# Eight weight sums made by accumulating DMAs instead of VectorE

## The chip, the cores and the metric

The kernel runs on one core of a Trainium2 chip. The metric is the device time of one execution in microseconds (us). Before the change it is 1120.05 us, the median of three runs (1119.95, 1120.05 and 1120.61).

A core has five engines that each work through a queue of their own in order: TensorE (PE, matrix products; its weight loads are shown as PEld), VectorE (DVE), ScalarE (ACT), GpSimd (POOL) and SyncE (SP). SP does no arithmetic here; it only issues DMAs. An instruction that waits for a semaphore holds back all that is behind it on its own engine.

## The reference

One decoder layer for 512 tokens of width 1024, in float32: a gated feed-forward network (FFN1), two attention mixers side by side, a second feed-forward network (FFN2), and a last norm.

```python
h = h + FFN_HALF * _swiglu(_rmsnorm(h, norm_ffn1[i]), ffn1_gate[i], ffn1_up[i], ffn1_down[i])
...                                # mixers
h = h + FFN_HALF * _swiglu(_rmsnorm(h, norm_ffn2[i]), ffn2_gate[i], ffn2_up[i], ffn2_down[i])
return _rmsnorm(h, norm_final)

def _swiglu(x, w_gate, w_up, w_down):
    return (jax.nn.silu(x @ w_gate) * (x @ w_up)) @ w_down
```

The inner width of both networks is 2816. The change concerns the second one's down projection, `ffn2_down`, a matrix of 2816 by 1024.

## The kernel before

**Split products.** Every float32 product is made of three matmuls on a high and a low part of each operand. A weight block (128 rows by 8 tiles of 128) is loaded by SP into a ring of four buffers named `raw` (line 152), ScalarE copies it to `whi` (line 160) and VectorE subtracts to make `wlo` (line 164). TensorE then spends 24 matmuls of 512 columns on a block. Blocks are used strictly in the order in which they are planned. `Weights.prep` issues the load of block i + 3 ahead of the split of block i, and the ring gives a `raw` buffer free when the split of the block four places earlier is done. So SP, which works in order, mostly stands waiting for VectorE's `wlo`.

**FFN1** runs from the start to about 375 us. It takes the 22 blocks of the inner width in three parts of 8, 8 and 6. In each part a loop over `f` makes the gate and up products (two weight blocks to a step, and `swiglu` between), then a loop over `d` makes the eight blocks of the down product.

**A seven-product scheme.** For the first two of these parts FFN2's down product is done with seven products of half blocks instead of eight. It needs sums of quarters of `ffn2_down`. Take a pair of 128-row blocks as a 2 by 2 arrangement b11, b12 (columns 0 to 511 and 512 to 1023 of the first row block) and b21, b22. Four combinations t1 to t4 are wanted of each pair. There are eight pairs. The combinations go to DRAM (`t_sums`) and are read back as weight blocks in FFN2's `down()` at about 800 to 1000 us, beside combinations of the left operand that `gated()` makes.

**Where the sums are made.** This is done ahead of time, in FFN1, by the generator `Weights.early`. The loops of `ffn` call `next(early)` once for each `f`, and at d = 2 and d = 5 of the first two down loops. Step n of it stores the result of item n - 2, loads item n, and works on item n - 1. Items 0 to 11 are weight blocks that are only split ahead (lines 110 and 111). Items 12 to 19 are the eight pairs:

- `load` (line 104): SP issues two DMAs of 512 KB into two `eraw` tiles (four buffers, so two items at a time);
- `work` (line 116): VectorE makes four subtractions of 128x512 into `ehi` and `elo`;
- `store` (line 126): SP issues four DMAs of 256 KB to DRAM.

The load, the work and the store of a step are emitted behind the `swiglu` of that `f`, or behind the addition of that `d`. On SP they stand in one queue with the `raw` loads of line 152. On GpSimd nothing runs between 39 and 349 us.

Of the kernel before, what the change touches and what calls it, by code (L numbers as in the profile page):

```python
# [8 lines left out]
F32 = mybir.dt.float32  # L9
F32R = mybir.dt.float32r  # L10
I32 = mybir.dt.int32
AF = mybir.ActivationFunctionType
OP = mybir.AluOpType
# [42 lines left out]
def f32(ap):  # L56
    return ap.bitcast(F32)


class Weights:  # L60
# [28 lines left out]
    def early(self, pool, sums):  # L89


        nc = self.nc
        order = sorted(self.stored)
        raw, out = {}, {}

        def load(n):
            if n < len(order):
                ap, nk = self.blocks[order[n]]
                raw[n] = [pool.tile([128, nk, 128], F32, name="eraw", bufs=4)]
                nc.sync.dma_start(raw[n][0], ap)  # L100
                return
            raw[n] = [pool.tile([128, 8, 128], F32, name="eraw", bufs=4) for _ in range(2)]
            for t, ap in zip(raw[n], sums[n - len(order)][0]):
                nc.sync.dma_start(flat(t), ap)

        def work(n):
            x, y = out[n] = [pool.tile([128, 8, 128], F32R, name=name) for name in ("ehi", "elo")]
            if n < len(order):
                src, = raw.pop(n)
                nc.scalar.copy(x, src)  # L110
                nc.vector.tensor_tensor(y, src, f32(x), op=OP.subtract)
                return
            (b11, b12), (b21, b22) = (halves(flat(t)) for t in raw.pop(n))
            (t1, t2), (t3, t4) = (halves(flat(f32(t))) for t in (x, y))
            for o, p, q in ((t1, b12, b11), (t2, b22, t1), (t3, b22, b12), (t4, t2, b21)):
                nc.vector.tensor_tensor(o, p, q, op=OP.subtract)

        def store(n):
            x, y = (f32(t) for t in out.pop(n))
            if n < len(order):  # L120
                for part, t in enumerate((x, y)):
                    nc.sync.dma_start(self.stored[order[n]][part], t)
                return
            places = sums[n - len(order)][1]
            for o, t in zip(places, (*halves(flat(x)), *halves(flat(y)))):
                nc.sync.dma_start(o, t)

        total = len(order) + len(sums)
        for n in range(total + 2):
            if n >= 2:  # L130
                store(n - 2)
            if n < total:
                load(n)
            if 1 <= n <= total:
                work(n - 1)
            yield
# [68 lines left out]
def flat(t):  # L205
    return t.rearrange("p a b -> p (a b)")


def halves(t):
    return t[:, :512], t[:, 512:]  # L210
# [159 lines left out]
def layer(ctx, tc, a, out):  # L370
    nc = tc.nc
    tensor, scalar, vector, gpsimd = nc.tensor, nc.scalar, nc.vector, nc.gpsimd
# [18 lines left out]
    def mm(out, lhsT, rhs, start, stop):  # L391
        tensor.matmul(out, lhsT, rhs, start=start, stop=stop)  # L392

    def split(hi, lo, src):
        scalar.copy(hi, src)  # L395
        vector.tensor_tensor(lo, src, f32(hi), op=OP.subtract)
# [276 lines left out]
    with pool("h1") as h_pool, pool("temp1", 2) as temp, pool("tables") as tables, ExitStack() as starting:  # L673
        start = starting.enter_context(pool("start"))
        h = h_pool.tile([128, KD, S], F32, name="h")
        x = start.tile([128, 4, D], F32, name="x")
# [110 lines left out]
    with ExitStack() as mixing:  # L787
# [47 lines left out]
        for k in range(KD):  # L835
            for t in range(4):
                o, ts = kcv_ps[t][:, 0], slice(t * 128, t * 128 + 128)
# [118 lines left out]
        class Turned:  # L956

            o = b = None
# [532 lines left out]
        h = h_pool.tile([128, KD, S], F32, name="h")  # L1491
# [8 lines left out]
        with pool("merge", 2, side="right") as mp:  # L1500
# [9 lines left out]
            for d in range(KD):  # L1510
# [16 lines left out]
                y, z = gates_z  # L1527
# [11 lines left out]
    with pool("temp3", 2) as temp, pool("end") as end:  # L1539
# [18 lines left out]
        def gated(pg, pu, j, pairs):  # L1558
            z = temp.tile([128, S], F32, name="z")
            vector.tensor_tensor(z, pg, r_b, op=OP.mult)  # L1560
            s = temp.tile([128, S], F32, name="s")
            scalar.activation(s, z, AF.Silu)
            t = temp.tile([128, S], F32, name="t")
            vector.tensor_tensor(t, pu, r_b, op=OP.mult)
            if not pairs:
                g = temp.tile([128, 8, 256], F32, name="g").rearrange("p m c -> p (m c)")[:, :S]
                vector.tensor_tensor(g, s, t, op=OP.mult)
                split(G[:, j], G[:, 8 + j], g)
                return
            if j % 2 == 0:  # L1570
                left["g"] = temp.tile([128, 8, 256], F32, name="g")
            g, p = left["g"], j // 2
            o = g[:, 1:3] if j % 2 else g[:, 0:8:7]
            vector.tensor_tensor(o, *(x.rearrange("p (i c) -> p i c", i=2) for x in (s, t)), op=OP.mult)
            if j % 2 == 0:
                return
            if j == 7:
                W.prep(W.pos + 3)
            hi, lo = left_hi[:, p], left["lo"][:, p]
            vector.tensor_tensor(g[:, 3], g[:, 7], g[:, 2], op=OP.add)  # L1580
            scalar.copy(hi[:, 0:4], g[:, 0:4])
            vector.tensor_tensor(g[:, 4], g[:, 3], g[:, 0], op=OP.subtract)
            vector.tensor_tensor(lo[:, 0:4], g[:, 0:4], f32(hi[:, 0:4]), op=OP.subtract)
            vector.tensor_tensor(g[:, 5], g[:, 0], g[:, 7], op=OP.subtract)
            vector.tensor_tensor(g[:, 6], g[:, 1], g[:, 4], op=OP.subtract)
            scalar.copy(hi[:, 4:7], g[:, 4:7])
            vector.tensor_tensor(lo[:, 4:7], g[:, 4:7], f32(hi[:, 4:7]), op=OP.subtract)

        def down():


            home = {1: "acc", 6: "acc", 7: "acc", 5: "o", 3: "o", 2: "s", 4: "s"}
            gets = {1: ((0, 0, 0.5),), 5: ((0, 1, 0.5), (1, 1, 0.5)), 2: ((0, 0, 0.5),), 6: (), 3: ((0, 1, 0.5),),
                    4: ((1, 0, -0.5),), 7: ()}
            more = {6: ((0, 1),), 7: ((1, 0), (1, 1))}
            banks = {}
            u = temp.tile([128, 2, 512], F32, name="u", bufs=1)
            for m, g in STEPS:
                if g == 0:
                    banks[m] = [psum.tile([128, 512], F32, name=home[m]) for _ in range(2)]  # L1600
                wh, wl = (w.rearrange("p (a b) c -> p a (b c)", a=2) for w in W.next())
                for t in range(2):
                    ps, c = banks[m][t], slice(t * 128, t * 128 + 128)
                    for q in range(2):
                        ah, al = (x[:, 2 * g + q, LEFT[m], c] for x in (left_hi, left["lo"]))
                        mm(ps, ah, wh[:, q], g == q == 0, False)
                        mm(ps, al, wh[:, q], False, False)
                        mm(ps, ah, wl[:, q], False, g == q == 1)
                    if g == 0:
                        continue  # L1610
                    if m == 1:
                        scalar.activation(u[:, t], ps, AF.Identity, scale=0.5)
                    if m in more:
                        vector.scalar_tensor_tensor(u[:, t], ps, 0.5, u[:, t], op0=OP.mult, op1=OP.add)
                    for i, k, by in gets[m]:
                        y = o_t[:, 2 * i + t, k * 512:k * 512 + 512]
                        vector.scalar_tensor_tensor(y, ps, by, y, op0=OP.mult, op1=OP.add)
                    for i, k in more.get(m, ()):
                        y = o_t[:, 2 * i + t, k * 512:k * 512 + 512]
                        vector.tensor_tensor(y, y, u[:, t], op=OP.add)  # L1620
            turn[0] = 0

        def residual(d):
# [70 lines left out]
        for third, (f0, f1) in enumerate(THIRDS):  # L1694
            for f in range(f0, f1):
                pg = acc(False)
                mm3(pg, W.next(), u_in, KD, col if f == 0 else None)
                pu = acc(False)
                mm3(pu, W.next(), u_in, KD, rows if f == 0 else None)
                if f < 2:  # L1700
                    for d in range(4 * f, 4 * f + 4):
                        residual(d)
                if f == 1:
                    make_room()
                if third == 2:
                    next(last)
                if third < 2 and f + 1 == f1:
                    W.prep(W.pos + 2)
                gated(pg, pu, f - f0, third < 2)
            if third < 2:  # L1710
                down()
# [27 lines left out]
```

## Time and profile before

| | |
|---|---|
| median of three runs | 1120.05 us |
| span of the profiled execution (first to last instruction) | 1118.3 us |
| what lies around the span, by the median | 1.75 us |
| PE busy | 1103.9 us (99%) |
| DVE busy | 696.0 us (62%) |
| ACT busy | 473.2 us (42%) |
| POOL busy | 155.3 us (14%) |
| granted TensorE clock, mean | 0.999 |

The profiled execution has no time of its own beside its span; the three runs are 1.65 to 2.31 us above that span.

How to read the lines: "L116" is line 116 of the kernel; "ehi<-eraw" is the tile written and the tile read; "x8" is how many there are. In a timeline the first number is the start in us from the start of the span and the second the duration. "DMA to landing" is the time from the issue of a DMA to its completion. SPq rows are DMAs that SP issues. In a table by stretches each engine has its busy us and, in brackets, its instructions; then the granted clock, the mean busy share of the 16 DMA engines, and what they moved in GB/s.

### The profile page before, as it was taken

How to read it: one execution, taken by the hardware profiler on the slowest of the kernel's cores; microseconds unless marked ns; L12 is line 12 of the kernel's file. 1: busy time of each engine (PE TensorE's matmuls, PEld its weight loads, DVE VectorE, ACT ScalarE, POOL GpSimd, SP SyncE). 2: the span in 40 equal slices, each digit the busy share in tenths (PEclk: the TensorE clock that was granted, in tenths of full speed). 3: DMA queues.
4: the chain of work that ended last, by engine and by line, in shares of the span. 5: the costliest groups of instructions: out<-in, count | busy, mean ns of one | idle time of the engine just before them, and what ended most of it. 6: DMA issues, size and time to landing. Idle time of an engine off the chain costs nothing.

```text
span 1118.3 us, 14946 instructions
## 1 busy us (share of the span) xinstructions
PE 1103.9 (99%) x5571; PEld 933.3 (83%) x5571; DVE 696.0 (62%) x1275; ACT 473.2 (42%) x890; POOL 155.3 (14%) x173
## 2 busy tenths in 40 slices
PE   9999999999999999999999999999999999999997
PEld 7888888888888999998888888888888888888876
DVE  5665447674656588896777546653667754685553
ACT  5444223321234456766666543434334322342332
POOL 0100000000001144644233422120000000000002
PEclk9999999999999999999999999999999999999999
DMA  7387557886745524224324255633234623354212
GB/s 232 95 245 249 184 175 239 286 276 208 240 143 151 140 79 116 76 76 142 123 93 144 70 162 162 173 87 111 76 113 144 194 79 112 113 178 124 90 61 76
DMA packets 202049, 163.17 MB, mean 146 GB/s; under 512 B 6836, under 2 KB 177656, under 8 KB 201976
## 3 DMA queue, kind: packets, MB, share of 16 engines
q1 hardware_dynamic: 199304, 157.87, 46.0%
q10 hardware_dynamic: 2672, 4.35, 1.0%
q8 instruction: 44, 0.72, 0.3%
q14 instruction: 29, 0.24, 0.1%
HBM read 133.88 MB, written 28.31 MB: 145 GB/s over the span
## 4 chain that ended last, share of the span: by engine, by line
PE 95%; DVE 2%; ACT 1%; issue 1%; POOL 0%; POOLq 0%; DVEq 0%; ACTq 0%
PE acc L392 37%; PE o L392 27%; PE s L392 27%; PE tp L1430 2%; DVE turn_a L1128 0%; PE tp L392 0%; PE tp L1056 0%; PE tp L721 0%; DVE wlo L164 0%; ACT whi L160 0%; PE tp L1627 0%; PE tp L988 0%; DVE s L1336 0%; POOL sqacc L581 0%; DVE sqacc L1173 0%
## 5 line engine op out<-in xcount | busy, mean ns | idle before, releaser
L164 DVE TENSOR_TENSOR wlo<-raw,whi 128x1024 fp32r<-128x1024 f32 (+2 forms) x189 | 215.5, 1168 | 40.0 <-ACT whi L160 39.8
L160 ACT CAST whi<-raw 128x1024 fp32r<-128x1024 f32 (+2 forms) x214 | 190.1, 919 | 109.0 <-PE acc L392 43.7
L392 PE MATMUL acc<-uh,whi 128*128 128x512 f32 x336 | 133.4, 397 | 0.7 <-ACT turn_a L1247 0.7
L392 PE MATMUL acc<-uh,wlo 128*128 128x512 f32 x336 | 131.3, 391 | 0.0
L392 PE MATMUL acc<-ul,whi 128*128 128x512 f32 x336 | 131.1, 390 | 0.0
L392 PE MATMUL o<-uh,whi 128*128 128x512 f32 x264 | 103.7, 393 | 0.4 <-ACT whi L726 0.4
L392 PE MATMUL o<-ul,whi 128*128 128x512 f32 x264 | 102.8, 390 | 0.0
L392 PE MATMUL o<-uh,wlo 128*128 128x512 f32 x264 | 102.8, 389 | 0.0
L392 PE MATMUL s<-uh,whi 128*128 128x512 f32 x232 | 90.5, 390 | 0.0
L392 PE MATMUL s<-uh,wlo 128*128 128x512 f32 x232 | 90.3, 389 | 0.0
L392 PE MATMUL s<-ul,whi 128*128 128x512 f32 x232 | 90.3, 389 | 0.0
L392 PEld LDWEIGHTS acc<-uh,wlo 128*128 128x128 f32 x336 | 63.1, 188 | 13.8 <-DVE wlo L164 0.4
L392 PEld LDWEIGHTS acc<-uh,whi 128*128 128x128 f32 x336 | 63.1, 188 | 12.9 <-ACT turn_a L1247 1.1
L392 PEld LDWEIGHTS acc<-ul,whi 128*128 128x128 f32 x336 | 63.2, 188 | 11.8
L581 POOL TENSOR_TENSOR sqacc<-sqacc,turn_a 128x512 f32<-128x512 f32 x14 | 18.2, 1300 | 371.0 <-ACT turn_a L580 371.0
L392 PE MATMUL acc<-whi,uh 128*128 128x256 f32 x224 | 65.5, 292 | 1.2 <-ACT whi L160 1.2
L392 PE MATMUL acc<-wlo,uh 128*128 128x256 f32 x224 | 63.3, 283 | 0.1
L392 PE MATMUL acc<-whi,ul 128*128 128x256 f32 x224 | 63.3, 283 | 0.0
L395 ACT CAST G<-g 128x512 fp32r<-128x512 f32 x28 | 17.4, 622 | 101.5 <-DVE g L633 72.3
L392 PEld LDWEIGHTS o<-uh,whi 128*128 128x128 f32 x264 | 49.6, 188 | 11.4 <-ACT whi L726 0.9
L392 PEld LDWEIGHTS o<-uh,wlo 128*128 128x128 f32 x264 | 49.6, 188 | 10.5
L392 PEld LDWEIGHTS o<-ul,whi 128*128 128x128 f32 x264 | 49.6, 188 | 10.2
(343 smaller groups left out, 2324.9 us busy)
## 6 DMA issues: line engine op xcount, KB each, us to landing
raw<-in_ffn_gate_dram SPq DMA_DIRECT2D x42, 512.0 KB, 4.0
raw<-in_ffn_up_dram SPq DMA_DIRECT2D x42, 512.0 KB, 5.2
raw<-in_ffn_down_dram SPq DMA_DIRECT2D x34, 512.0 KB, 5.1
raw<-in_w_in_dram SPq DMA_DIRECT2D x20, 512.0 KB, 4.3
eraw<-in_ffn_down_dram SPq DMA_DIRECT2D x16, 512.0 KB, 7.0
raw<-t SPq DMA_DIRECT2D x16, 512.0 KB, 3.3
eraw<-in_w_in_dram SPq DMA_DIRECT2D x12, 512.0 KB, 7.6
early<-ehi SPq DMA_DIRECT2D x12, 512.0 KB, 5.3
```

What stands on the lines that cost most here:

```text
L160: self.nc.scalar.copy(self.place(i)[0][:, k0:k1], self.raw[i][:, k0:k1])
L164: engine.tensor_tensor(lo, self.raw[i][:, k0:k1], f32(hi), op=OP.subtract)
L392: tensor.matmul(out, lhsT, rhs, start=start, stop=stop)
L395: scalar.copy(hi, src)
L581: gpsimd.tensor_tensor(sqacc, sqacc, sq, op=OP.add)
L1430: tensor.transpose(ps[:w, hd], u.p[:, hd, kb * w:kb * w + w], ident)
```

## The change

The four combinations are formed by DMAs that add to what stands at their destination (`accum_op=OP.add`). They are issued by GpSimd, as are the four stores. They can only add, so the combinations get other signs, and the left operands of FFN2 get the signs to match.

Of a pair, SP now loads the first row block with one DMA (512 KB) into one `eraw` tile and the second row block with two (256 KB each), halves exchanged, into another. So the tiles hold b11, b12 and b22, b21. Then GpSimd issues, in this order: t1 = b11 + b12, with b12 read from DRAM; t3 = b12 + b22, with b22 read from DRAM; t2 = b22 + t1, with t1 read from the tile; t4 = b21 + t2, with t2 read from the tile. The results replace the loaded data, and the stores read from the `eraw` tiles.

```diff
-            raw[n] = [pool.tile([128, 8, 128], F32, name="eraw", bufs=4) for _ in range(2)]
-            for t, ap in zip(raw[n], sums[n - len(order)][0]):
-                nc.sync.dma_start(flat(t), ap)
+            raw[n] = [pool.tile([128, 1024], F32, name="eraw", bufs=4) for _ in range(2)]
+            row1, row2 = sums[n - len(order)][0]
+            nc.sync.dma_start(raw[n][0], row1)
+            for k in range(2):
+                nc.sync.dma_start(halves(raw[n][1])[k], halves(row2)[1 - k])
...
-            (b11, b12), (b21, b22) = (halves(flat(t)) for t in raw.pop(n))
-            (t1, t2), (t3, t4) = (halves(flat(f32(t))) for t in (x, y))
-            for o, p, q in ((t1, b12, b11), (t2, b22, t1), (t3, b22, b12), (t4, t2, b21)):
-                nc.vector.tensor_tensor(o, p, q, op=OP.subtract)
+            t1, t3, t2, t4 = (h for t in raw[n] for h in halves(t))
+            row1, row2 = sums[n - len(order)][0]
+            for o, i in ((t1, halves(row1)[1]), (t3, halves(row2)[1]), (t2, t1), (t4, t2)):
+                nc.gpsimd.dma_start(o, i, accum_op=OP.add)
...
-            places = sums[n - len(order)][1]
-            for o, t in zip(places, (*halves(flat(x)), *halves(flat(y)))):
-                nc.sync.dma_start(o, t)
+            t1, t3, t2, t4 = (h for t in raw.pop(n) for h in halves(t))
+            for o, t in zip(sums[n - len(order)][1], (t1, t2, t3, t4)):
+                nc.gpsimd.dma_start(o, t)
...
-            vector.tensor_tensor(g[:, 3], g[:, 7], g[:, 2], op=OP.add)
+            vector.tensor_tensor(g[:, 3], g[:, 7], g[:, 2], op=OP.subtract)
...
-            vector.tensor_tensor(g[:, 6], g[:, 1], g[:, 4], op=OP.subtract)
+            vector.scalar_tensor_tensor(g[:, 6], g[:, 1], -1.0, g[:, 4], op0=OP.mult, op1=OP.subtract)
...
-            gets = {1: ((0, 0, 0.5),), 5: ((0, 1, 0.5), (1, 1, 0.5)), 2: ((0, 0, 0.5),), 6: (), 3: ((0, 1, 0.5),),
-                    4: ((1, 0, -0.5),), 7: ()}
-            more = {6: ((0, 1),), 7: ((1, 0), (1, 1))}
+            gets = {1: ((0, 0, 0.5),), 5: ((0, 1, 0.5), (1, 1, 0.5)), 2: ((0, 0, 0.5),), 6: (), 3: ((0, 1, -0.5),),
+                    4: ((1, 0, 0.5),), 7: ()}
+            more = {6: ((0, 1, OP.subtract),), 7: ((1, 0, OP.add), (1, 1, OP.subtract))}
```

More of the change, by code (lines that the diff above doesn't have):

```diff
@@ L101, in load @@
                 return
-            raw[n] = [pool.tile([128, 8, 128], F32, name="eraw", bufs=4) for _ in range(2)]
-            for t, ap in zip(raw[n], sums[n - len(order)][0]):
-                nc.sync.dma_start(flat(t), ap)
+            raw[n] = [pool.tile([128, 1024], F32, name="eraw", bufs=4) for _ in range(2)]
[3 more added lines that the diff above has]
+                nc.sync.dma_start(halves(raw[n][1])[k], halves(row2)[1 - k])
         def work(n):
-            x, y = out[n] = [pool.tile([128, 8, 128], F32R, name=name) for name in ("ehi", "elo")]
             if n < len(order):
+                x, y = out[n] = [pool.tile([128, 8, 128], F32R, name=name) for name in ("ehi", "elo")]
                 src, = raw.pop(n)
@@ L112, in work @@
                 return
-            (b11, b12), (b21, b22) = (halves(flat(t)) for t in raw.pop(n))
-            (t1, t2), (t3, t4) = (halves(flat(f32(t))) for t in (x, y))
-            for o, p, q in ((t1, b12, b11), (t2, b22, t1), (t3, b22, b12), (t4, t2, b21)):
-                nc.vector.tensor_tensor(o, p, q, op=OP.subtract)
+            t1, t3, t2, t4 = (h for t in raw[n] for h in halves(t))
+            row1, row2 = sums[n - len(order)][0]
+            for o, i in ((t1, halves(row1)[1]), (t3, halves(row2)[1]), (t2, t1), (t4, t2)):
+                nc.gpsimd.dma_start(o, i, accum_op=OP.add)
         def store(n):
-            x, y = (f32(t) for t in out.pop(n))
             if n < len(order):
+                x, y = (f32(t) for t in out.pop(n))
                 for part, t in enumerate((x, y)):
@@ L1617, in down @@
                         vector.scalar_tensor_tensor(y, ps, by, y, op0=OP.mult, op1=OP.add)
-                    for i, k in more.get(m, ()):
+                    for i, k, op in more.get(m, ()):
                         y = o_t[:, 2 * i + t, k * 512:k * 512 + 512]
-                        vector.tensor_tensor(y, y, u[:, t], op=OP.add)
+                        vector.tensor_tensor(y, y, u[:, t], op=op)
             turn[0] = 0
```

## The prediction

> **What bounds the kernel now.** I read the page's shares first, then the stretches in which the sums are made, then the waits there.
>
> ```profile
> span 1118.3 us, 14946 instructions
> PE 1103.9 (99%) x5571; PEld 933.3 (83%) x5571; DVE 696.0 (62%) x1275; ACT 473.2 (42%) x890; POOL 155.3 (14%) x173
> ```
>
> ```profile
> core 0: us, PE busy (x) PEld busy (x) DVE busy (x) ACT busy (x) POOL busy (x), PEclk, DMA share, GB/s
> 194.00:230.00 36.00, 36.00 (x161) 29.81 (x160) 23.60 (x38) 11.05 (x14) 0.00 (x0) 1.00 0.83 279
> 230.00:257.00 27.00, 27.00 (x121) 22.37 (x120) 17.02 (x26) 6.86 (x8) 0.00 (x0) 1.00 0.82 269
> 257.00:297.00 40.00, 40.00 (x178) 33.15 (x177) 21.41 (x30) 9.30 (x14) 0.00 (x0) 1.00 0.62 201
> 297.00:316.00 19.00, 19.00 (x85) 15.73 (x84) 13.50 (x18) 6.03 (x8) 0.00 (x0) 1.00 0.76 248
> ```
>
> The stretches run from the first load of a pair to its last store. TensorE is busy for the whole of each at a granted clock of 1.00, and GpSimd does nothing. The longest wait that TensorE or its weight loads have for VectorE's split in all of FFN1 is this one:
>
> ```profile
> PEld acc L392 <- DVE wlo L164: 0.4, 1, 0.4
> ```
>
> So relief for VectorE has at most 0.4 us to win there. The DMA engines are the busiest helper, up to 0.83. What can change is a loss: whether weights still come in time through SP's queue.
>
> ```profile
> SPq L152 <- DVE wlo L164: 82.4, 17, 11.3
> ```
>
> That is SP's own wait between 190 and 325 us: it stands waiting until a raw buffer is free. In this kernel SP runs as far ahead as four buffers let it, and no further.
>
> **VectorE's part goes.** One sum before, and the split behind it:
>
> ```profile
> 308.85 0.69 DVE L116 TENSOR_TENSOR ehi<-eraw 128x512 f32<-128x512 f32 x1
> 309.57 0.69 DVE L116 TENSOR_TENSOR ehi<-eraw,ehi 128x512 f32<-128x512 f32 x1
> 310.18 0.68 DVE L116 TENSOR_TENSOR elo<-eraw 128x512 f32<-128x512 f32 x1
> 310.79 0.69 DVE L116 TENSOR_TENSOR elo<-ehi,eraw 128x512 f32<-128x512 f32 x1
> 311.39 2.35 DVE L164 TENSOR_TENSOR wlo<-raw,whi 128x1024 fp32r<-128x1024 f32 x2
> ```
>
> From 308.85 to 311.39 is 2.54 us; eight sums make 20.3 us of VectorE's 696.0. I cost the gain at nothing, since TensorE covers all of it. Late behind it would be the weights' arrival.
>
> **FFN2's signs.** Four add or subtract changes keep their form. The eight g[:, 6] become a three-operand form. Nearest rows: the instruction now, and a three-operand one of twice the width, beside a subtraction of that width at 0.69 above.
>
> ```profile
> L1585 DVE TENSOR_TENSOR g<-g x8: 415/418/420, 786.8 to 978.6; 128x256 f32<-128x256 f32 x8
> 246.23 0.69 DVE L664 SCALAR_TENSOR_TENSOR h<-o,h 128x512 f32<-128x512 f32 x1 [3.61 <-PE o L392]
> ```
>
> Equal price, so nothing.
>
> **DMAs move.** SP issued 2 loads and 4 stores a sum and now issues 3 loads, 24 instead of 48. GpSimd issues 8 a sum, 64 in all: 32 accumulates and 32 stores. SP's shorter list is worth nothing by itself, since SP waits 82.4 us anyway.
>
> **The new wait.** An eraw tile is now in use until its stores have landed. So SP's load of a pair waits for the stores of the pair two before, and behind that load on SP stand the raw loads. GpSimd's queue is a chain within a sum: t1 and t3 are issued, t2 waits for t1 to land, t4 for t2, the last store for t4, and the next sum's t1 stands behind that store. With A for one accumulate from issue to landing and one issue between sums, GpSimd needs 3A + 0.7 us for a sum. The 0.7 is SP's row for issuing (median 709 ns), as GpSimd issues no DMA before. The issue time's bounds, 0.46 and 1.40 us, move the period by less than 0.7 and the answer by five times that, under 3.5 us, inside the range below.
>
> ```profile
> L104 SPq DMA_DIRECT2D eraw<-in_ffn_down_dram x16: 456/709/1398, 193.9 to 295.9; - x16
> DMA to landing us min/median/max: 6.4/7.0/7.4
> ```
>
> ```profile
> L126 SPq DMA_DIRECT2D t<-ehi x16: 422/566/887, 216.0 to 313.7; - x16
> DMA to landing us min/median/max: 3.9/5.0/6.6
> ```
>
> ```profile
> L152 SPq DMA_DIRECT2D raw<-in_ffn_up_dram x7: 368/396/823, 196.8 to 305.1; - x7
> DMA to landing us min/median/max: 3.7/6.0/8.5
> ```
>
> ```profile
> hd<-h SPq DMA_DIRECT2D x8, 256.0 KB, 2.4
> ```
>
> **The price of A.** No accumulate stands in this trace. From below: 2.4 us, a plain 256 KB in a quiet stretch. From above: 8.5 us, the slowest 512 KB raw load here (the landing line covers all raw loads from 190 to 330 us). An accumulate of 256 KB must read the destination besides the source, 512 KB in all, so its nearest row is a 512 KB transfer in the same crowded stretch: 6.0 us. I take A = 6.0; a sum takes 18.7 us.
>
> **The sum.** SP's queue before, and where TensorE begins the block that the last raw load brings:
>
> ```profile
> 193.94 2.72 SPq L104 DMA_DIRECT2D eraw<-in_ffn_down_dram  x2
> 256.46 1.72 SPq L104 DMA_DIRECT2D eraw<-in_ffn_down_dram  x2
> 258.96 0.38 SPq L152 DMA_DIRECT2D raw<-in_ffn_up_dram  x1
> 295.12 1.41 SPq L104 DMA_DIRECT2D eraw<-in_ffn_down_dram  x2
> 296.63 0.42 SPq L152 DMA_DIRECT2D raw<-in_ffn_up_dram  x1
> 308.12 2.00 ACT L160 CAST whi<-raw 128x1024 fp32r<-128x1024 f32 x2
> 322.19 0.39 PE L392 MATMUL o<-uh,whi 128*128 128x512 f32 x1
> ```
>
> The first pair is loaded at 193.94 and landed 7.0 later, at 200.9. Its t4 lands at 200.9 + 18.0 = 218.9, the n-th after it 18.7 n later, and the stores 5.0 after that. The eighth load needs the sixth sum's stores: 218.9 + 5 x 18.7 + 5.0 = 317.4. Before, it was issued at 295.12: 22.3 us late. The block behind it was issued at 296.63, is the second of the pair cast at 308.12, and is first multiplied at 322.19. Of those 25.6 us it needs 6.0 to land, and 1.0 and 1.2 for its two splits (halves of the rows of 2.00 and 2.35), 8.2; 17.3 us are slack. TensorE stalls for 22.3 - 17.3 = 5.0 us. The sixth load (256.46) comes at 280.0, 23.5 late, but its raw block (258.96) is first multiplied at 289.55:
>
> ```profile
> 289.55 0.39 PE L392 MATMUL o<-uh,whi 128*128 128x512 f32 x1
> ```
>
> That is 30.6 us, slack 22.4, a stall of 1.1 which the 5.0 contains. So the span grows from 1118.3 to 1123.3 us. The runs' median lies 1.75 above that span; the same around the new span gives 1125 us, 0.4% slower. The point of turning is A = 5.7 (5.0/18 below 6.0), and each microsecond of A beyond it costs 18 us, three landings in each of six sums. At 8.5 it would be 50 us, 1170; at 2.4 nothing.
>
> **What lies behind it on GpSimd.** Its next work is the first of eight additions of squares:
>
> ```profile
> 349.01 1.34 POOL L581 TENSOR_TENSOR sqacc<-sqacc,turn_a 128x512 f32<-128x512 f32 x1 [309.69 <-ACT turn_a L580]
> ```
>
> The eighth sum's t4 lands at 218.9 + 7 x 18.7 = 349.8; the addition is then due at 354. This costs nothing, barely.
>
> **The rivals.** *Hidden.* With A below 5.7 us SP's lateness stays inside the slack, and the time is 1120. For it: a plain 256 KB store lands in 5.0 us at the median here and in 2.4 in quiet, two accumulates of a sum have both ends on chip, and a delayed SP queue makes the stretch less crowded. Against it: the double reading, and GpSimd's unknown time for issuing. On the price of such a DMA there is a rule in the Trainium skill, "DMA: Bandwidth & Descriptors", section "Anatomy of one DMA — SWDGE (gpsimd) path": about 2.0 us and the bytes at 436 GB/s. By it a plain 256 KB takes an estimated 2.6 us, the sum would be 8.5 us a pair, and this rival would hold with room. No run here shows a DMA of GpSimd's yet.
>
> *The DMA engines run full.* The four stretches carry a share of 0.83, 0.82, 0.62 and 0.76, so 36 x 0.17 + 27 x 0.18 + 40 x 0.38 + 19 x 0.24 = 31 us of all sixteen are free. A share of 0.83 moves 279 GB/s, so a full one 336. The accumulates add 32 x 0.262 MB = 8.4 MB, 25 us, if they cost what a copy does; 50 if double and 75 if triple. Single fits. Triple is 44 us over; less the 17.3 of slack, 27 us, 1147. Against it: the free share lies unevenly but the last stretch to 340 us is quiet. This is what the Trainium skill warns of, on the same page, section "Issuing engines are not separate DMA queues": DMAs of GpSimd's, SP's and ScalarE's queues run on the same 16 engines and interleave. The trace before cannot test it, having nothing on GpSimd's queue.
>
> *Faster.* Only if VectorE held TensorE somewhere; the 0.4 us above is all that the waits give, 1119.6.
>
> **How the numbers follow.** Forecast (SP waits on the chain, A from 5.7 to 8): 0.42, its own range 1121 to 1160. Hidden: 0.41. Engines full: 0.14. Faster: 0.03. About 0.2%, 2.2 us, is what a measurement of this kernel can tell from no change. Then faster 0.03, the same 0.41, slower 0.56. The range goes from 1119, under which only the last case lies, to 1160, which is A = 7.9.
>
> **What would show it.** In the changed kernel the L116 rows of VectorE are gone. SP waits at L104 for DMAs rather than at L152 for wlo, with the eighth pair's load near 317 us. TensorE has idle time ahead of blocks at 290 to 330 us, released by wlo or whi, and in no other place. An accumulate's landing is the number to look at: below 5.7 us TensorE stays without a gap and I am wrong by 5 us; near 8 I am wrong by 40. The prediction also fails if GpSimd's issue takes several microseconds a DMA, for then stores too lengthen the chain.

## The result

The changed kernel takes 1127.55 us, the median of four runs (1125.45, 1127.41, 1127.69 and 1130.25). Before it was 1120.05. The ratio is 1.0068 with a 95% interval of 1.0053 to 1.0082: it is slower by 0.7%. The profiled execution is the longest of the four: its time is 1130.25 us and its span 1128.5, 10.2 us more than the span before.

The page of the changed kernel, first the busy times, then the shares of the chain that ended last:

```profile
span 1128.5 us, 15012 instructions
PE 1108.7 (98%) x5571; PEld 935.2 (83%) x5571; DVE 675.8 (60%) x1243; ACT 473.2 (42%) x890; POOL 201.1 (18%) x237
...
PE 85%; DMA 6%; DVE 3%; issue 3%; ACT 1%; POOL 1%; SPq 0%; POOLq 0%; DVEq 0%; ACTq 0%
```

VectorE has lost 20.2 us of work (696.0 to 675.8), almost exactly the 20.3 of the eight sums, and the kernel is not faster for it. TensorE still does 5571 matmuls, but 6% of the chain that sets the end is now DMA. The busy PE time has grown by 4.8 us with the same matmuls, so some of them ran more slowly.

The table by stretches shows where. Its columns are the busy us of each engine (instructions in brackets), the granted clock, the share of the 16 DMA engines, and GB/s. The stretch in which the sums are made:

```profile
core 0: us, PE busy (x) PEld busy (x) DVE busy (x) ACT busy (x) POOL busy (x), PEclk, DMA share, GB/s
200.00:250.00 50.00, 50.00 (x222) 41.39 (x221) 25.61 (x41) 12.92 (x16) 14.41 (x19) 1.00 0.95 260
250.00:300.00 50.00, 48.32 (x211) 38.77 (x210) 18.09 (x24) 11.87 (x16) 16.43 (x23) 1.00 0.99 257
300.00:350.00 50.00, 47.80 (x204) 38.78 (x203) 22.87 (x29) 14.86 (x20) 14.90 (x21) 0.97 0.95 243
```

From 250 to 350 us TensorE has idle time, in a stretch where it had none. The last row before was:

```profile
300.00:350.00 50.00, 50.00 (x222) 41.44 (x221) 28.46 (x37) 15.70 (x22) 0.98 (x1) 1.00 0.51 156
```

In the last row after, the clock is 0.97 as well. Cut finer, the same columns:

```profile
323.00:326.70 3.70, 2.09 (x10) 1.39 (x8) 0.00 (x0) 0.92 (x1) 0.15 (x1) 1.00 1.14 280
326.70:330.20 3.50, 2.91 (x7) 1.97 (x8) 3.12 (x4) 0.79 (x3) 2.36 (x4) 0.59 1.19 292
```

In the first of these TensorE stands idle for 1.6 us at full clock. In the second it works, but at a granted clock of 0.59. (The DMA share adds up the packets' times and counts each packet in the stretch in which it starts, so it can come out above 1.)

Lining up the same matmul in the two traces gives the whole difference step by step. By the matmul that started at 322.6 us before, the changed kernel is 5.50 us late, gathered between 273 and 323 us of the kernel before in several small stalls. A spell of 3.41 us at half clock follows and makes it 6.82. At 479 us one wait adds 1.02 (7.84), and a second spell at half clock brings it to 9.02. At the last matmul it is 9.15. The stretch from the start of the last matmul to the end of the span is 8.38 us where it was 7.36, another 1.02. Together that is the 10.2 us. The other three runs left no trace, so how their smaller losses divide isn't known.

**What TensorE waited for at 326 us.** SP's waits in the same window as before, 190 to 325 us, with the total, the count and the longest:

```profile
SPq L104 <- DMA t<-eraw: 64.3, 12, 11.5
SPq L154 <- DVE wlo L166: 15.3, 3, 6.1
```

Before, SP waited 82.4 us for VectorE's `wlo`. Now it waits mostly for GpSimd's stores to land. The eighth pair's loads, and the raw load that stands behind them, in SP's timeline (start, duration):

```profile
314.94 0.34 SPq L104 DMA_DIRECT2D eraw<-in_ffn_down_dram  x1
316.01 1.10 SPq L106 DMA_DIRECT2D eraw<-in_ffn_down_dram  x2
317.21 0.56 SPq L154 DMA_DIRECT2D raw<-in_ffn_up_dram  x1
```

and the other end of that raw load, in the timelines of ScalarE, VectorE and TensorE (in brackets the idle time ahead of the instruction and what ended it):

```profile
325.78 1.04 ACT L162 CAST whi<-raw 128x1024 fp32r<-128x1024 f32 x1 [11.28 <-DMA raw<-in_ffn_up_dram]
326.86 1.23 DVE L166 TENSOR_TENSOR wlo<-raw,whi 128x1024 fp32r<-128x1024 f32 x1 [11.10 <-ACT whi L162]
326.88 0.50 PE L394 MATMUL o<-uh,whi 128*128 128x512 f32 x1 [1.79 <-ACT whi L162]
328.14 0.80 PE L394 MATMUL o<-uh,wlo 128*128 128x512 f32 x1 [0.41 <-DVE wlo L166]
```

All four engines stand in one row: the DMA lands, ScalarE starts at once after 11.28 us of nothing, VectorE after it, TensorE after ScalarE. The matmul at 328.14 takes 0.80 us where 0.39 is usual. That is the half clock.

**Why SP's load was late.** GpSimd's timeline for one pair, the sixth:

```profile
296.56 1.86 POOL L118 DMA_DIRECT2D eraw<-in_ffn_down_dram  x2
301.48 0.86 POOL L118 DMA_DIRECT2D eraw<-eraw  x1 [3.06 <-DMA eraw<-in_ffn_down_dram]
309.23 0.86 POOL L118 DMA_DIRECT2D eraw<-eraw  x1 [6.89 <-DMA eraw<-eraw]
309.77 1.97 POOL L128 DMA_DIRECT2D t<-eraw  x3
312.91 0.55 POOL L128 DMA_DIRECT2D t<-eraw  x1 [1.17 <-DMA eraw<-eraw]
313.45 1.86 POOL L118 DMA_DIRECT2D eraw<-in_ffn_down_dram  x2
```

t1 and t3 are issued at 296.56; t2 follows only when t1 has landed, t4 when t2 has, the last store (that of t4) when t4 has, and the next pair stands behind it. The three landings take 4.9, 7.8 and 3.7 us from issue to issue. The prices over all pairs, by the view of that line (count, then ns of one issue at least, median and most):

```profile
L118 POOL DMA_DIRECT2D eraw<-in_ffn_down_dram x16: 896/1161/1289, 201.8 to 333.1; - x16
L118 POOL DMA_DIRECT2D eraw<-eraw x16: 858/862/871, 206.6 to 347.3; - x16
DMA to landing us min/median/max: 3.4/6.9/9.2
```

### The profile page after: what moved, and what is told of

It is laid out like the page before. It is cut to its first block, busy times and chain, and to the rows that moved or that the text cites. A ratio compares the mean times of both kernels' runs of the same rounds, so it can differ in the third digit from the quotient of the medians.

```text
span 1128.5 us, 15012 instructions
## 1 busy us (share of the span) xinstructions
PE 1108.7 (98%) x5571; PEld 935.2 (83%) x5571; DVE 675.8 (60%) x1243; ACT 473.2 (42%) x890; POOL 201.1 (18%) x237
## 4 chain that ended last, share of the span: by engine, by line
PE 85%; DMA 6%; DVE 3%; issue 3%; ACT 1%; POOL 1%; SPq 0%; POOLq 0%; DVEq 0%; ACTq 0%
PE acc L394 33%; PE o L394 24%; PE s L394 23%; DMA eraw<-eraw 5%; PE tp L1432 2%; DMA raw<-in_ffn_up_dram 1%; POOL eraw L118 1%; PE tp L394 1%; DVE turn_a L1130 0%; DVE wlo L166 0%; PE tp L1058 0%; ACT whi L162 0%; PE tp L723 0%; PE tp L1629 0%; DMA t<-eraw 0%
## 5 line engine op out<-in xcount | busy, mean ns | idle before, releaser
L1667 POOL TENSOR_TENSOR o_t<-o_t,g_b 128x512 f32<-128x512 f32 (+1 forms) x5 | 5.9, 1176 | 334.1 <-ACT z L1661 334.1
```

Source lines behind the costliest of these rows:

```text
L1667: gpsimd.tensor_tensor(y, y, g_b[:, cs], op=OP.mult)
```

## The experiments

The theory is that of the prediction: a pair takes GpSimd three landings one after the other, the stores of the pair two before therefore land late, SP waits for them, and the raw loads behind it on SP come late. The main rival is that the DMA engines are simply full. Each kernel was timed in rounds with the kernel before, whose medians were 1120.03 and 1120.00 us on the two chips used.

**More buffers.** Six `eraw` buffers in place of four: the same DMAs, but SP's load of a pair waits for the stores of the pair three before.

```diff
-            raw[n] = [pool.tile([128, 1024], F32, name="eraw", bufs=4) for _ in range(2)]
+            raw[n] = [pool.tile([128, 1024], F32, name="eraw", bufs=6) for _ in range(2)]
```

> The changed kernel with six eraw buffers instead of four; the accumulates, their order and their bytes stay. Buffer wait (my theory: SP's load of a pair is held until the stores of the pair two before have landed, and the raw loads behind it come later than their slack): a load now waits for the pair three before, one chain of 18.7 us earlier, so the eighth load is about 3 us late instead of 20, inside the slack of 17. TensorE has no gap between 250 and 340 us and never a spell at half clock there; 1121 us, the 1 us left being the longer end (next kernels). Full engines (rival: the sixteen DMA engines cannot carry the accumulates beside the weights, share 0.95 to 0.99 from 200 to 350 us): taking the wait away does not make room, raw loads still land late, TensorE keeps most of its 5.5 us of gaps; 1125 to 1128 us.

Measured: 1121.87 us (1121.49 to 1123.83), ratio 1.0020 [1.0011, 1.0029]. The table by stretches of this kernel, its waits of SP, and the eighth pair's load:

```profile
200.00:250.00 50.00, 50.00 (x222) 41.44 (x221) 26.94 (x42) 15.07 (x18) 13.98 (x19) 1.00 1.04 294
250.00:300.00 50.00, 50.00 (x223) 41.40 (x222) 20.62 (x27) 12.69 (x17) 15.41 (x23) 1.00 0.95 255
300.00:350.00 50.00, 50.00 (x222) 41.43 (x221) 24.01 (x31) 15.81 (x22) 14.83 (x21) 1.00 0.95 235
```

```profile
SPq L104 <- DMA t<-eraw: 36.0, 9, 8.2
```

```profile
301.52 0.34 SPq L104 DMA_DIRECT2D eraw<-in_ffn_down_dram  x1
```

TensorE is busy for 50.00 of 50 us in all three, with a DMA share of 0.95 to 1.04, as full as in the changed kernel. A bandwidth limit would have stayed. The wait for the buffer is the cause of FFN1's loss, and SP may wait 36 us in total without harm: what counts is how late a load has become against the slack of the block behind it. The eighth load goes out 6.4 us later than in the kernel before (301.52 against 295.12), in the changed kernel 19.8 us later. The kernel remains 1.8 us slower, which is not in FFN1.

**No chain.** t2 and t4 add a quarter from DRAM, so no accumulate waits for another's result.

```diff
-            for o, i in ((t1, halves(row1)[1]), (t3, halves(row2)[1]), (t2, t1), (t4, t2)):
+            for o, i in ((t1, halves(row1)[1]), (t3, halves(row2)[1]), (t2, halves(row1)[0]), (t4, halves(row1)[1])):
```

> The changed kernel with t2 and t4 each adding a half of the first row block from DRAM instead of the sum before it, so t2 and t4 are not the sums wanted; 32 accumulates of 256 KB as before, none waiting for another. Buffer wait: a sum takes one landing and about 4 us of issuing instead of three landings, 11 us instead of 18.7, and SP's loads are late by under 5 us; no gap, 1121 us. Full engines: the same bytes through the same engines, more crowded if anything; gaps stay, 1125 to 1128 us or more.

Measured: 1123.3 us (1121.45 to 1123.61), ratio 1.0024 [1.0014, 1.0033]. Two stretches:

```profile
200.00:250.00 50.00, 50.00 (x222) 41.40 (x222) 25.95 (x41) 13.14 (x17) 21.21 (x28) 1.00 1.06 300
250.00:300.00 50.00, 50.00 (x222) 41.42 (x221) 21.59 (x27) 14.86 (x19) 17.30 (x24) 1.00 1.10 308
```

The engines carry more than in the changed kernel (300 and 308 GB/s) and one accumulate takes longer to land, 8.2 us at the median against 6.9. Still TensorE has no gap, and the eighth load goes out at 295.52 us, within half a microsecond of the kernel before. So not the number or the price of the accumulates does the harm, but that they wait for each other.

**A fifth accumulate.** t4 adds t2 twice, which puts one more landing into each pair's chain and 12.5% more DMAs on GpSimd.

```diff
-            for o, i in ((t1, halves(row1)[1]), (t3, halves(row2)[1]), (t2, t1), (t4, t2)):
+            for o, i in ((t1, halves(row1)[1]), (t3, halves(row2)[1]), (t2, t1), (t4, t2), (t4, t2)):
```

> The changed kernel with a fifth accumulate per pair, t4 adding t2 a second time behind the first (so t4 is not the sum wanted). Buffer wait: the chain of a pair grows by one landing of about 6 us, from 18.7 to 25, and the eighth load by six times that, 36 us later, all of it beyond the slack; TensorE stalls some 35 us more, 1155 to 1170 us. Full engines: eight accumulates more at 1.6 us of all engines each are 13 us, so at most 1141 us.

Measured: 1156.02 us (1155.01 to 1156.75), ratio 1.032 [1.0306, 1.0334], 28.5 us over the changed kernel. The eighth load and two stretches:

```profile
339.89 0.34 SPq L104 DMA_DIRECT2D eraw<-in_ffn_down_dram  x1
```

```profile
250.00:300.00 50.00, 41.16 (x163) 32.32 (x162) 10.08 (x11) 6.27 (x6) 15.52 (x21) 0.90 0.90 229
300.00:350.00 50.00, 38.21 (x159) 30.03 (x157) 15.98 (x22) 10.77 (x16) 13.22 (x18) 0.90 0.88 225
```

The eighth load moved by 25 us (314.94 to 339.89), not by the 36 that was expected: the added link made a pair about 4 us longer, not 6. The profiled span moved by 26.5 us (1128.5 to 1155.0) and the median by 28.5. The matmul that started at 322.6 us in the kernel before is 31.3 us late here and 5.5 in the changed kernel, 25.8 us more. So past the slack, the lateness of the chain is paid about one for one. The clock is 0.90 in both rows, but the spells of slow clock ahead of that block add little to this: TensorE stands idle for 11.7 us just before it, waiting for its load. The DMA share is lower than in the changed kernel, 0.90 and 0.88: the engines carry less while TensorE loses most. That ends the rival of full engines.

**Copies instead of accumulates.** The same chain with plain copies, so that no sums are made.

```diff
-                nc.gpsimd.dma_start(o, i, accum_op=OP.add)
+                nc.gpsimd.dma_start(o, i)
```

> The changed kernel with plain copies in the place of the accumulates, same sources, destinations, queue and order, so the copies stand where sums should. Buffer wait: a 256 KB copy of GpSimd's lands in about 4.3 us (its stores' median) against 6.9 for an accumulate, so a pair takes 14 us instead of 18.7, the eighth load is not late, no gap in FFN1, and what stays is the price of 64 DMAs on GpSimd, 1121.9 us as with six buffers. If it is not the accumulating but the queue that makes the chain long, copies land in 6 to 7 us too and the time stays at 1127.

Measured: 1123.2 us (1121.64 to 1123.77), ratio 1.0024 [1.0014, 1.0033]. The chained copies' prices, and GpSimd's first and last issue of a pair:

```profile
L118 POOL DMA_DIRECT2D eraw<-eraw x16: 536/536/538, 206.1 to 330.8; - x16
DMA to landing us min/median/max: 2.3/5.1/7.2
```

```profile
202.10 1.33 POOL L118 DMA_DIRECT2D eraw<-in_ffn_down_dram  x2 [162.28 <-DMA eraw<-in_ffn_down_dram]
...
321.28 1.07 POOL L118 DMA_DIRECT2D eraw<-in_ffn_down_dram  x2
```

A pair takes (321.28 - 202.10) / 7 = 17.0 us, not the 14 that was expected: a chained copy lands in 5.1 us here. The accumulating itself, its longer issue included, then costs 1.7 of the changed kernel's 18.7 us a pair, and three landings in a row the rest. The eighth load goes out at 304.12, 9.0 us later than before, inside the slack. TensorE has no gap in FFN1 at 17.0 us a pair and has them at 18.7, which brackets the turning point that the prediction worked out (3 x 5.7 + 0.7 = 17.8 us).

**VectorE without the sums, no accumulates.** Only the loads and GpSimd's stores are left of a pair.

```diff
-            for o, i in ((t1, halves(row1)[1]), (t3, halves(row2)[1]), (t2, t1), (t4, t2)):
-                nc.gpsimd.dma_start(o, i, accum_op=OP.add)
```

> The changed kernel without its 32 accumulates: the row blocks are loaded and stored as they are, no sums are made by any engine. 32 DMAs of GpSimd's are left. Buffer wait: no chain, so no late load, no gap in FFN1. VectorE makes no sums here and made them in the kernel with GpSimd's stores alone (1122.24 us); if VectorE's 20 us are worth nothing, as predicted, the two are equal: 1121 to 1122 us. If VectorE's relief is worth something, it is below 1120.0. The last drain of GpSimd's, which was 0.64 us with 0 DMAs, 3.27 with 32, 5.88 with 64 and 6.54 with 72, is 3.3 us again.

**VectorE with the sums, GpSimd with the stores.** One edit to the kernel before:

```diff
-                nc.sync.dma_start(o, t)
+                nc.gpsimd.dma_start(o, t)
```

> The kernel before, with only its 32 stores of the sums issued by GpSimd instead of SP; VectorE makes the sums. If the longer end of the changed kernel (GpSimd's last drain 5.88 us instead of 0.64, the span's end 8.4 instead of 7.4 us behind the last matmul) comes from GpSimd having issued DMAs at all: the same long drain here, 1121.0 us, no gap in FFN1. If it comes from accumulates or something else: 1120.0 us and a drain of 0.6 us.

Measured: 1122.33 us (1120.46 to 1122.81; ratio 1.0016 [1.0007, 1.0024]) without any sums, and 1122.24 us (1120.6 to 1122.96; 1.0015 [1.0006, 1.0024]) with all sums on VectorE. The two have the same stores on GpSimd and differ by VectorE's 20.3 us, and their times are the same (they ran on different chips, on which the kernel before agrees within 0.03 us). They are the same, too, within each of the two groups into which the runs of both fall: 1120.46 to 1120.89 and 1120.60 to 1120.98 in the lower, 1122.22 to 1122.81 and 1122.24 to 1122.96 in the upper (the last section says what parts them). The relief of VectorE is worth nothing. Neither has a gap in FFN1. But both stand above the kernel before, which the theory of the chain doesn't explain, and the drain at the end is longer in both than before. The last drain of GpSimd's queue (the third figure, in ns) in four kernels: the kernel before,

```profile
L1735 POOLq DRAIN  x3: 34/78/642, 1112.6 to 1118.0; - x3
```

the stores alone on GpSimd (32 DMAs),

```profile
L1735 POOLq DRAIN  x3: 40/93/3274, 1113.5 to 1118.9; - x3
```

the changed kernel (64),

```profile
L1737 POOLq DRAIN  x3: 46/102/5884, 1121.8 to 1128.2; - x3
```

and the fifth accumulate (72):

```profile
L1737 POOLq DRAIN  x3: 46/93/6536, 1147.7 to 1154.8; - x3
```

642, 3274, 5884 and 6536 ns lie on a line: 0.64 us and 0.082 us for each DMA that GpSimd issued at any time in the kernel. At 32 it is hidden beside the last output (last matmul to end of span 7.38 us, before 7.36). At 64 that stretch is 8.38, at 72 9.02. This is the 1.0 us at the end.

**A control without DMAs on GpSimd.** The kernel before with the pairs' stores from ScalarE:

```diff
-                nc.sync.dma_start(o, t)
+                nc.scalar.dma_start(o, t)
```

> The kernel before, with its 32 stores of the sums issued by ScalarE: a control beside the one whose stores GpSimd issues (1122.24 us), with no DMA on GpSimd. If the 0.8 to 1.0 us that all kernels with GpSimd DMAs lose at 479 us (VectorE's 128x2 addition there takes 1.14 instead of 0.16 us beside a running GpSimd instruction) and the rest of the 2 us come from GpSimd's DMAs, this one is at 1120.0 us. If any small shift of FFN1's DMAs brings them, it is at 1121 to 1122 us as well.

Measured: 1120.81 us (1120.55 to 1122.5), ratio 1.0013 [1.0004, 1.0022]. The drain is 0.64 us and the end 7.35, as before, but the loss at 479 us is there: the one wait is 1.0 us longer. The place in the kernel before, in the timelines of GpSimd and VectorE and in its waits:

```profile
472.64 1.28 POOL L164 TENSOR_TENSOR wlo<-raw,whi 128x512 fp32r<-128x512 f32 x1
473.81 0.16 DVE L1340 TENSOR_TENSOR e<-m,sink 128x2 f32<-128x2 f32 x1
```

```profile
PE s L392 <- ACT pbuf L1344: 0.8, 1, 0.8
```

and in the control:

```profile
473.50 1.28 POOL L164 TENSOR_TENSOR wlo<-raw,whi 128x512 fp32r<-128x512 f32 x1
473.66 1.14 DVE L1340 TENSOR_TENSOR e<-m,sink 128x2 f32<-128x2 f32 x1
```

```profile
PE s L392 <- ACT pbuf L1344: 1.8, 1, 1.8
```

The VectorE instruction of two columns takes 1.14 us in place of 0.16. It stands in the chain that leads to ScalarE's `pbuf`, for which TensorE now waits 1.8 us and not 0.8. The changed kernel has the same instruction at 1.15 us and the same wait of 1.8. Beside it GpSimd makes a row of 128x512 subtractions. In the control VectorE's instruction starts 0.16 us into one of them and ends as that one ends, at 474.8. In the kernel before it starts 1.17 us into a subtraction of 1.28 us, and also ends as that one ends, at 473.9 to 474.0. In all nine versions other than the kernel before, the control among them, it starts 0.15 to 0.19 us into a subtraction and takes 1.13 to 1.15 us. The Trainium skill states, in "SBUF — State Buffer", section "Who interferes with whom", that VectorE and GpSimd share a pair of ports under an exclusive lock, and that a VectorE instruction with two SBUF inputs contends with a GpSimd instruction that reads SBUF. The rows agree with it. So this part belongs to the phase of the two engines, which every edit of FFN1's queues here moved. Why it moves was not tried.

**Buffers and SP's stores together.** The accumulates stay, with six buffers and the stores back on SP, one step later so that SP needn't wait for t4.

```diff
-            raw[n] = [pool.tile([128, 1024], F32, name="eraw", bufs=4) for _ in range(2)]
+            raw[n] = [pool.tile([128, 1024], F32, name="eraw", bufs=6) for _ in range(2)]
...
-                nc.gpsimd.dma_start(o, t)
+                nc.sync.dma_start(o, t)
...
-        for n in range(total + 2):
-            if n >= 2:
+        for n in range(total + 3):
+            if 2 <= n < len(order) + 2:
                 store(n - 2)
...
+            if n >= len(order) + 3:
+                store(n - 3)
```

> The changed kernel with six eraw buffers and the stores of the sums back on SP, one step later than before so that SP seldom waits for the chain; only the accumulates stay on GpSimd, 32 DMAs. The version that keeps the sums off VectorE at the least price. GpSimd's last drain 3.3 us, hidden behind the output; SP's stores wait for t4 of a pair three steps back, late by at most 12 to 19 us, about the slack. 1120.5 to 1122 us; nothing below the kernel before, as VectorE's relief is worth nothing. With gaps in FFN1 it would be 1123 to 1126.

Measured: 1122.33 us (1120.51 to 1122.93), ratio 1.0017 [1.0008, 1.0026]. FFN1 has no gap, the drain is down to 3.27 us, and the end is 7.39. The three lowest of its eleven runs lie at 1120.51 to 1120.73, the seven lowest of the version with six buffers and 64 DMAs on GpSimd at 1121.49 to 1122.19. Their middles, 1120.68 and 1121.78, are 1.1 us apart, about the end's 8.38 against 7.39. Both losses of the change, the chain's and the end's, are thus taken away one after the other. What is left is the phase at 479 us and, in the other eight runs, some 1.8 us more (the last section). No version was faster than the kernel before.

## Why the prediction came out

The forecast was 1125 us, the median is 1127.55. The mechanism is the one forecast; its terms one by one:

- **VectorE's relief is worth nothing.** So it is (the pair of experiments with and without sums). FFN2's signs cost nothing, too: the three-operand form has the same duration as the add before, 418 ns.

```profile
L1587 DVE SCALAR_TENSOR_TENSOR g<-g x8: 415/418/420, 796.0 to 987.8; 128x256 f32<-128x256 f32 x8
```

- **The chain, 18.7 us a pair.** The first issue of a pair is at 201.80 us and the eighth at 332.52, so a pair takes 130.72 / 7 = 18.67 us.

```profile
201.80 2.03 POOL L118 DMA_DIRECT2D eraw<-in_ffn_down_dram  x2 [162.48 <-DMA eraw<-in_ffn_down_dram]
...
332.52 1.86 POOL L118 DMA_DIRECT2D eraw<-in_ffn_down_dram  x2
```

  The close agreement holds for the sum more than for its parts, and in this much it is luck. The median landing of an accumulate was 6.9 us, not 6.0, but that counts t3, which is not in the chain. The three links took 5.2 (t1), 7.5 (t2) and 4.6 us (t4) on average over the eight pairs, 17.3 us and not 18.0, and what lies between them about 1.4, not 0.7. t2 and t4 have the same shape; t2 is issued while t3 is still under way, but whether it stands behind t3 was not tried. The reason given for the 6.0, that an accumulate reads twice, accounts for a small part of it: plain copies in the same chain landed in 5.1 us and made 17.0 us a pair. The Trainium skill's fit in "DMA: Bandwidth & Descriptors", section "Anatomy of one DMA — SWDGE (gpsimd) path", gave an estimated 2.6 us for 256 KB. In this stretch, with the engines at a share near 1, GpSimd's plain 256 KB took 4.3 us as a store and 5.1 as a copy at the median, so here the measurement decides against it.

```profile
t<-eraw POOLq DMA_DIRECT2D x32, 256.0 KB, 4.3
```

- **The eighth load at 317.4 us.** Its first DMA went out at 314.94. That one doesn't wait for t4's store, as the prediction had it, since its tile holds t1 and t3; the second tile's two wait for it and went out from 316.01. The sixth pair's t4 landed at 312.6 (forecast 312.4); its store took about 3 us, not 5.0. The raw load behind it was 20.6 us late (296.63 to 317.21), not 22.3.
- **Slack 17.3 us, stall 5.0.** The late raw load took 8.6 us to land, not 6.0, so there was less slack, about 15. Lateness and slack were both over by some 2 us, and the stall came out at 5.5. The sixth load's stall was forecast as 1.1 and contained in this; by 296 us of the kernel before the traces show 2.7, contained as well. The first 0.8 of it came at 273 us, ahead of the 290 to 330 us that the prediction named.
- **GpSimd's later work.** The first addition of squares was to come at 354 us or a little sooner; it started at 355.86, on time for TensorE, which was itself 6.8 us late.
- **What the sum lacked.** Three terms, 4.5 of the profiled execution's 10.2 us: the clock, which fell to half behind a stall in two places (1.3 and 1.2 us), the phase at 479 us (1.0), and GpSimd's longer drain (1.0). None was in the sum, since it took the time outside FFN1 as unchanged and a stall as costing its own length. With only the last two added to the 5.0 us, the forecast would have been 1127. How the median run's loss divides isn't known, so that this lies near 1127.55 shows nothing by itself.
- **The rivals.** "Hidden" holds below the turning point, as the copies at 17.0 us a pair show, but accumulates don't lie below it. "Engines full" falls: at shares up to 1.10 TensorE had no gap once the buffer wait was gone. The 31 us of free engine time that its price was set against are no bound, then.

## What to carry to other kernels

Work that moves to a DMA queue takes up the buffer from load to store, and a chain of dependent DMAs costs a landing for each link (4.6 to 7.5 us here on average, for 256 KB). What must be compared is how late this makes the loads ahead of the weights with the slack of the block behind them, not busy shares: the queue could wait 36 us in all without harm, and TensorE lost 5.5 us when a load came out 20 us late. Two more buffers brought that to 6.4 us, found by asking which wait ends last. Relieving an engine that no critical wait names is worth nothing, here 20 us of it.

## What was not expected of the hardware

- The last drain of GpSimd's queue grows by 0.082 us for each DMA that GpSimd has issued, 0.64 us at none to 6.54 at 72, and shows in the time once it outlasts the last output.
- An accumulating DMA from tile to tile costs GpSimd 0.86 us to issue, against 0.54 for a copy of the same shape.
- The granted clock fell to half for 3.41 us behind idle stretches of only 1.8 us on TensorE, in some executions and not in others. At the wait for `pbuf` all nine versions have the same gap of 1.77 us in their traces (the kernel before has 0.79 and no spell); some are followed by a spell and some, the control above among them, are not. The runs of most of the small variants lie in two groups some 1.7 us apart (the control at 1120.55 to 1120.81 and at 1122.23 to 1122.5). The traces tell most of what parts them. The four profiled executions of the small variants that lie in an upper group (six buffers, no accumulates, copies, buffers and SP's stores together) each have one such spell between 480 and 486 us, and the three in a lower group (no chain, sums on VectorE with GpSimd's stores, the control) have none. From that gap to 483 us of the kernel before the first four lose 1.2 to 1.3 us, where the other three make up 0.2. What decides whether a spell follows isn't shown.
